# Attention steps of a head pair and one query tile, in a chain of two transformer blocks

## The chip, the core and the metric

The kernel runs on one core of a Trainium2 chip. Its engines are named as in the profile: PE (TensorE: matmuls and transposes; PEld is its loading of weights), DVE (VectorE), ACT (ScalarE), POOL (GpSimd) and SP (SyncE, which here only issues loads of weights). The metric is the time of one execution on the device in microseconds; less is better.

## The reference

Two blocks in a chain, all in fp32, D = 1024, batch 1. The first has 272 tokens (16 meta tokens and 256 of a 4 x 64 grid) and two layers, each a feed-forward part, a mixer, and another feed-forward part:

```
h = concat([meta, x])                                   # 16 + 256 tokens
for i in range(2):
    f1 = swiglu(rmsnorm(h, g[0]), gate, up, down);      h = h + 0.5 * rmsnorm(f1, g[1])
    hn = rmsnorm(h, g[2])
    m  = neighborhood_attention(hn) if i == 0 else diff_attention(hn)
    h  = h + rmsnorm(m, g[3])
    f2 = swiglu(rmsnorm(h, g[4]), ...);                 h = h + 0.5 * rmsnorm(f2, g[5])

def neighborhood_attention(h):                          # 16 heads of 64
    q, k, v = h @ w_qkv + b_qkv;  q = q * 64 ** -0.5
    # meta queries see the meta keys only
    om = softmax(qm @ km.T + meta_bias) @ vm
    # a grid query sees a window of 4 rows x 16 columns, and the meta keys
    og = softmax([q @ k_window.T + rpb, q @ km.T + meta_bias]) @ [v_window, vm]
    return concat([om, og]) @ w_o + b_o
```

The differential attention has 8 heads with two softmaxes each over all 272 keys; the values meet the difference of the two. The second block sees the 256 grid tokens. Its mixer computes, from one projection, attention with 8 heads of 64 in blocks of 256 keys, which for 256 tokens is plain causal attention, and beside it an mLSTM with 4 heads; an MLP with a squared ReLU follows.

## The kernel before

**Projections.** Activations lie transposed, features on the partitions and tokens in the columns. Each projection is made of products of 128 x 128 weights with 272 (or 256) columns, in three parts: high times high, low times high, high times low (`mm3`, L362 to L364). `Weights` brings the weights in: a raw load `wr` (SP), its high part `wh` (ACT, L122), and its low part `wl`, the difference of the two (L134), a *split* from here on, 128 x 1024 elements. The engine of the splits is `W.engine`. After each gemm, `W.pump()` issues up to two splits, and copies `wh` for later ones. `split` (L390) makes the high and low parts of an output in the same way, with the low part always on DVE.

**Mixers.** `mixer` runs the projections of q, k and v, two gemms per weight pair. The attention is a generator: it goes a piece further at k = 2 and k = 5 in each gemm and after each pump (`bg`). So the order of the code sets the order on every engine; the engines run it in order. A step u = (head pair, head) of `na_attention` does the following, for one head and both query tiles of 128:

- `scores(u)`: products of 64 partitions (the head's half) with 272 columns (L903), mask and row maximum on DVE (L856), exponentials on ACT;
- `weights(u)`: reciprocals of the sums and the scaling of the weights on DVE (L914, L915);
- `turn(u - 2)`: transposes on PE (L924) into PSUM, copied by ACT into `PT`, a ring of two buffers;
- `values(hp)`, every second step: the outputs of a head pair (L937), and before them those of its meta queries (L933), which wait for `ptm` (L981), the turned weights of the meta queries.

The meta queries of two head pairs are worked on together, one piece in each of three steps (`meta_scores`, `meta_weights` with L973, `meta_turn`). The window mask is added to the table of biases on POOL (`mask_bias`, 128 x 1536 elements a time). The products of projections, scores, values and half of the turns take turns in six PSUM buffers. `ready` tells `proj_out`, the output projection, which head pairs are complete.

The differential attention has its own steps (scores L1106, DVE L856, weights L1114 to L1118, values L1134, turned values `vs` L836). In the hybrid layer the order of gemms is written out as `plan`; `gates` (L1232, L1236) and the mLSTM run beside it, and `causal_attention` has the same steps as above: scores L1393, turns L1418, values L1426 to L1428; the query tile 0 sees 128 keys, the tile 1 sees 256. Rotary positions of q and k end in L1378 and L1379, the mLSTM's q in L1323.

**Engine of the splits.** It is POOL from the mixers' third gemm (`if 2 * n + q == 2`) and from the hybrid layer's `plan` on; `proj_out` sets it back to DVE (L652).

Of the kernel before, what the change touches and what calls it, by code (L numbers as in the profile page):

```python
# [13 lines left out]
AF = mybir.ActivationFunctionType  # L14
# [6 lines left out]
NM = 16  # L21
T = S + NM
# [153 lines left out]
def block_kernel(ctx: ExitStack, tc: tile.TileContext, a, out):  # L176
# [459 lines left out]
    def proj_out(post, x, order=range(8)):  # L636
# [15 lines left out]
        W.engine = dve  # L652
# [211 lines left out]
    ring = []  # L864
# [30 lines left out]
    def na_attention():  # L895
        vp, P, PT, em, ptm = {}, {}, {}, {}, {}
# [12 lines left out]

        def weights(u):  # L910
            for qt in range(2):
                e, sm = P[u, qt]
# [3 lines left out]
                P[u, qt] = e  # L916
# [467 lines left out]
    def causal_attention():  # L1384
        P, PT = {}, {}

        def scores(u):
            hp, b = divmod(u, 2)
            s = slice(64 * b, 64 * b + 64)
            for qt in range(2):  # L1390
# [4 lines left out]
                dve.tensor_tensor_reduce(out=lg[:, 0:n], in0=ps[:, 0:n], in1=causal[:, 256 - n:256], scale=1.0,  # L1395
# [5 lines left out]
                P[u, qt] = e, sm  # L1401

        def weights(u):
            for qt in range(2):
                n = 128 * (qt + 1)
                e, sm = P[u, qt]
# [3 lines left out]
                P[u, qt] = e  # L1410

        def turn(u):
            PT[u] = ring[0].tile()[:, 0:512].rearrange("p (k q) -> p k q", k=2)
            for qt in range(2):
                q = P.pop((u, qt))
                p = (ps_s if qt else ps_t)((128, 2, 128))
                for k in range(qt + 1):
                    pe.transpose(p[:, k, :], q[:, k * 128:k * 128 + 128], ident)  # L1418
                act.activation(PT[u][:, 0:qt + 1, qt * 128:qt * 128 + 128], p[:, 0:qt + 1, :], AF.Copy)
# [28 lines left out]
    W.engine = pool  # L1448
# [158 lines left out]
```

## Time and profile before

| | |
|---|---|
| median of 3 runs (lowest to highest) | 1474.24 us (1468.12 to 1475.06) |
| the profiled execution: own time, span | 1474.2 us, 1472.4 us |
| mean granted clock of PE | 0.991 |
| PE busy | 1438.7 us (98%), 10996 records |
| PEld busy | 1373.3 us (93%) |
| DVE busy | 907.2 us (62%), 1776 records |
| ACT busy | 752.8 us (51%) |
| POOL busy | 321.1 us (22%), 223 records |

The span runs from the first to the last instruction. Busy time is that in which an engine has a record running; a matmul of fp32 data leaves two records or more. The granted clock is a share of the full 2.4 GHz. 368 splits run on DVE (446.4 us) and 66 on POOL (159.9 us). The neighborhood mixer lies at about 243 to 352 us, the differential one at 815 to 927, the hybrid one at 1135 to 1265; nearly all the rest is feed-forward.

### The profile page before, as it was taken

What the parts mean: (1) busy time and instruction counts of PE and PEld (TensorE: products, weight loads), DVE (VectorE), ACT (ScalarE), POOL (GpSimd) and SP (SyncE); (2) the same over time, 40 slices, a digit from 0 to 9 for tenths busy, and PEclk for the clock granted to TensorE, in tenths of its full rate; (3) what the DMA queues carried; (4) which work ended last, traced back from release to release, by engine and by line L of the source; (5) the groups of instructions that cost most, each with busy time, mean ns of one, the idle gap of its engine ahead of it and who ended that gap; (6) DMA issues with size and microseconds to landing.
All of it is one profiled execution on the core that took longest, in us unless ns stands there. A gap on an engine that the chain in (4) does not pass through costs nothing.

```text
span 1472.4 us, 27036 instructions
## 1 busy us (share of the span) xinstructions
PE 1438.7 (98%) x10996; PEld 1373.3 (93%) x10996; DVE 907.2 (62%) x1776; ACT 752.8 (51%) x1327; POOL 321.1 (22%) x223
## 2 busy tenths in 40 slices
PE   9999999899999999999999899999999998999998
PEld 8999998788999999999999799999999887999886
DVE  6777448864775544765545755686645767596542
ACT  4554445555654444554444466564444555576541
POOL 3424002452021200121100455022200655000000
PEclk9999999999999999999999999999999899999999
DMA  7887554422385555265553433275554533265651
GB/s 235 253 250 202 171 183 129 116 86 87 93 269 177 171 175 193 90 226 172 166 179 115 146 113 115 87 230 188 178 186 137 173 115 112 90 193 183 213 188 40
DMA packets 231707, 236.42 MB, mean 161 GB/s; under 512 B 17825, under 2 KB 221798, under 8 KB 231390
## 3 DMA queue, kind: packets, MB, share of 16 engines
q1 hardware_dynamic: 230750, 229.63, 49.4%
q0 software_dynamic: 688, 4.99, 1.1%
q8 instruction: 87, 1.43, 0.4%
q14 instruction: 38, 0.31, 0.1%
q10 hardware_dynamic: 144, 0.07, 0.0%
HBM read 233.60 MB, written 5.13 MB: 162 GB/s over the span
## 4 chain that ended last, share of the span: by engine, by line
PE 74%; DVE 4%; ACT 1%; issue 0%; POOL 0%; DVEq 0%; POOLq 0%; ACTq 0%
PE pm L362 19%; PE pm L364 19%; PE pm L363 19%; PE ps L1531 2%; PE ps L1530 2%; PE ps L1532 2%; PE pm L475 2%; PE pm L471 1%; PE pm L472 1%; PE ps L1134 1%; PE pt L313 1%; PE ps L1106 1%; PE ps L937 0%; PE pm L445 0%; DVE hb L566 0%
## 5 line engine op out<-in xcount | busy, mean ns | idle before, releaser
L362 PE MATMUL pm<-xh,wh 128*128 128x272 f32 (+1 forms) x1992 | 584.2, 293 | 0.4 <-DVE s L856 0.4
L364 PE MATMUL pm<-xh,wl 128*128 128x272 f32 (+1 forms) x1992 | 572.1, 287 | 0.0
L363 PE MATMUL pm<-xl,wh 128*128 128x272 f32 (+1 forms) x1992 | 570.8, 287 | 0.0
L122 ACT ACTIVATE wh<-wr 128x1024 fp32r<-128x1024 f32 (+2 forms) x433 | 443.6, 1033 | 201.9 <-PE pm L363 121.8
L134 DVE TENSOR_TENSOR wl<-wr,wh 128x1024 fp32r<-128x1024 f32 (+2 forms) x368 | 446.4, 1221 | 123.9 <-ACT wh L122 123.0
L362 PEld LDWEIGHTS pm<-xh,wh 128*128 128x128 f32 x1992 | 378.3, 190 | 14.1 <-issue 10.9
L364 PEld LDWEIGHTS pm<-xh,wl 128*128 128x128 f32 x1992 | 378.0, 190 | 0.0
L363 PEld LDWEIGHTS pm<-xl,wh 128*128 128x128 f32 x1992 | 377.9, 190 | 0.1
L364 PE MATMUL pm<-mh,wl 128*128 128x272 f32 (+1 forms) x704 | 202.2, 287 | 0.0
L362 PE MATMUL pm<-mh,wh 128*128 128x272 f32 (+1 forms) x704 | 202.1, 287 | 0.0
L363 PE MATMUL pm<-ml,wh 128*128 128x272 f32 (+1 forms) x704 | 201.5, 286 | 0.0
L134 POOL TENSOR_TENSOR wl<-wr,wh 128x1024 fp32r<-128x1024 f32 x66 | 159.9, 2430 | 91.7 <-ACT wh L122 79.8
L599 POOL TENSOR_TENSOR sr<-sl,rb 128x272 f32<-128x272 f32 (+1 forms) x88 | 106.3, 1212 | 320.3 <-ACT sl L597 320.3
L364 PEld LDWEIGHTS pm<-mh,wl 128*128 128x128 f32 x704 | 132.6, 188 | 0.0
L363 PEld LDWEIGHTS pm<-ml,wh 128*128 128x128 f32 x704 | 132.6, 188 | 0.0
L362 PEld LDWEIGHTS pm<-mh,wh 128*128 128x128 f32 x704 | 132.5, 188 | 0.0
L318 POOL TENSOR_TENSOR s<-s,mhalf 128x3 f32<-128x3 f32 (+1 forms) x15 | 11.9, 796 | 504.8 <-DVE s L331 372.8
L389 ACT ACTIVATE mh<-m 128x272 fp32r<-128x272 f32 (+1 forms) x88 | 37.7, 428 | 120.5 <-DVE m L604 120.3
L604 DVE TENSOR_TENSOR m<-pm,sr 128x272 f32<-128x272 f32 (+1 forms) x88 | 38.2, 434 | 77.7 <-PE pm L364 72.0
L597 ACT ACTIVATE sl<-gq 128x272 f32<-128x272 f32 (+1 forms) x88 | 37.0, 428 | 89.3 <-DVE gq L595 88.7
L595 DVE TENSOR_TENSOR gq<-pm,rb 128x272 f32<-128x272 f32 (+1 forms) x88 | 37.5, 434 | 71.4 <-PE pm L364 63.6
L357 DVE TENSOR_TENSOR accf<-accf,sq 128x272 f32<-128x272 f32 (+1 forms) x42 | 18.3, 435 | 83.0 <-ACT sq L356 82.8
(343 smaller groups left out, 1912.0 us busy)
## 6 DMA issues: line engine op xcount, KB each, us to landing
wr<-in_ffn_w_gate_dram SPq DMA_DIRECT2D x43, 1024.0 KB
wr<-in_ffn_w_up_dram SPq DMA_DIRECT2D x43, 1024.0 KB
wr<-in_ffn_w_down_dram SPq DMA_DIRECT2D x32, 1024.0 KB
wr<-in_w_up_dram SPq DMA_DIRECT2D x16, 1024.0 KB
wr<-in_w_down_dram SPq DMA_DIRECT2D x16, 1024.0 KB
wr<-in_ffn_w_down_dram SPq DMA_DIRECT2D x16, 768.0 KB
wr<-in_na_w_qkv_dram SPq DMA_DIRECT2D x12, 1024.0 KB
wr<-in_da_w_qkv_dram SPq DMA_DIRECT2D x12, 1024.0 KB
```

The source lines that it names most:

```text
L122: self.nc.scalar.activation(hi, w, AF.Copy)
L134: engine.tensor_tensor(lo, w, hi.bitcast(F32), op=OP.subtract)
L362: pe.matmul(ps, wh[:, k, :], xh[:, j, cols], start=start, stop=False)
L363: pe.matmul(ps, wh[:, k, :], xl[:, j, cols], start=False, stop=False)
L364: pe.matmul(ps, wl[:, k, :], xh[:, j, cols], start=False, stop=stop)
L389: act.activation(hi, src, AF.Copy)
L475: pe.matmul(ps[q][:, c], w[q][0][:, k, :], norm.xl[:, k, c], start=False, stop=k == 7)
L595: dve.tensor_tensor(t[:, c], ps[:, c], norm.rb[:, c], op=OP.mult)
L597: act.activation(s[:, c], t[:, c], AF.Silu)
L599: pool.tensor_tensor(s2[:, c], s[:, c], norm.rb[:, c], op=OP.mult)
L604: dve.tensor_tensor(t[:, c], ps[:, c], gated.pop(f)[:, c], op=OP.mult)
L1530: pe.matmul(ps, xh, wh, start=start and k == 0, stop=False)
```

## The change

It does four things. (1) A step of `na_attention` and `causal_attention` is now u = (head pair, query tile): the products of the pair's two heads, which lie on partitions 0 to 63 and 64 to 127, stand next to each other, and `PT` holds one tile of both heads. (2) The values go tile by tile, the heads in turn: in the neighborhood layer twelve products of 128 columns where there were six of 256. (3) The outputs of the meta queries leave `values` and get a step of their own, `meta_values(g)`, with a split of their own; `part_done` marks a head pair ready after both. Their other pieces come one step later. (4) The three lines that set `W.engine` are gone, so that it stays DVE; of POOL's 66 splits 64 move there, and two in the first feed-forward stage, which name POOL themselves, stay.

```diff
-        W.engine = dve
...
+        def part_done(hp):
+            parts[hp] = parts.get(hp, 0) + 1
+            if parts[hp] == 2:
+                ready.add(hp)
 
         def scores(u):
-            hp, b = divmod(u, 2)
-            g = u // 4
-            for qt in range(2):
-                ps = ps_s()
-                pe.matmul(ps, kq[64 * b:64 * b + 64, hp % 4, QT[qt]], kq[64 * b:64 * b + 64, 4 + hp % 4, :],
-                          start=True, stop=True)
-                s0 = 2 - 2 * qt
-                e, r = softmax(ps, [(slice(0, NM), mb[:, u * NM:u * NM + NM]),
-                                    (GRID, bt[g][:, u % 4, s0:s0 + 4, :].rearrange("p s k -> p (s k)"))], T)
-                P[u, qt] = e, r
+            hp, qt = divmod(u, 2)
+            ps = [ps_s() for _ in range(2)]
+            for b in range(2):
+                s = slice(64 * b, 64 * b + 64)
+                pe.matmul(ps[b], kq[s, hp % 4, QT[qt]], kq[s, 4 + hp % 4, :], start=True, stop=True)
+            s0 = 2 - 2 * qt
+            for b in range(2):
+                hd = 2 * hp + b
+                bias = bt[hp // 2][:, hd % 4, s0:s0 + 4, :].rearrange("p s k -> p (s k)")
+                P[u, b] = softmax(ps[b], [(slice(0, NM), mb[:, hd * NM:hd * NM + NM]), (GRID, bias)], T)
...
         def turn(u):
-            PT[u] = ring[0].tile().rearrange("p (k q) -> p k q", k=3)
-            for qt in range(2):
-                q = P.pop((u, qt))
-                p = (ps_s if qt else ps_t)((128, 3, 128))
+            PT[u] = ring[0].tile().rearrange("p (b k q) -> p b k q", b=2, k=3)
+            for b in range(2):
+                q = P.pop((u, b))
+                p = (ps_s if b else ps_t)((128, 3, 128))
                 for i, x in enumerate((0, 128, 144)):
                     pe.transpose(p[:, i, :], q[:, x:x + 128], ident)
-                act.activation(PT[u][:, :, qt * 128:qt * 128 + 128], p, AF.Copy)
+                act.activation(PT[u][:, b], p, AF.Copy)
 
         def values(hp):
             o = ps_s()
-            v = vp.pop(hp)
-            for b in range(2):
-                s = slice(64 * b, 64 * b + 64)
-                i = 2 * (hp % 2) + b
-                pe.matmul(o[s, 0:NM], v[0:NM, 0, s], ptm[hp // 2][:, i * 16:i * 16 + 16], start=True, stop=True)
-            for k in range(3):
-                for b in range(2):
-                    s = slice(64 * b, 64 * b + 64)
-                    pe.matmul(o[s, NM:T], v[:, k, s], PT[2 * hp + b][:, k, :], start=k == 0, stop=k == 2)
-            split(Oh[:, hp, :], Ol[:, hp, :], o)
-            ready.add(hp)
+            for qt in range(2):
+                for k in range(3):
+                    for b in range(2):
+                        s = slice(64 * b, 64 * b + 64)
+                        pe.matmul(o[s, QT[qt]], vp[hp][:, k, s], PT[2 * hp + qt][:, b, k, :],
+                                  start=k == 0, stop=k == 2)
+            split(Oh[:, hp, GRID], Ol[:, hp, GRID], o[:, GRID])
+            part_done(hp)
...
+        def meta_values(g):
+            o = ps_s((128, 2, NM))
+            for n in range(2):
+                for b in range(2):
+                    s = slice(64 * b, 64 * b + 64)
+                    i = 2 * n + b
+                    pe.matmul(o[s, n, :], vp[2 * g + n][0:NM, 0, s], ptm[g][:, i * 16:i * 16 + 16],
+                              start=True, stop=True)
+            x = slice(2 * g, 2 * g + 2)
+            split(Oh[:, x, 0:NM], Ol[:, x, 0:NM], o)
+            for n in range(2):
+                part_done(2 * g + n)
+
         for u in range(16 + 3):
             if u % 2 == 0 and u >= 4:
                 values(u // 2 - 2)
@@ -989,13 +1004,15 @@
             if u < 16:
...
-                if u % 4 == 1:
+                if u % 4 == 2:
                     meta_scores(u // 4)
                 yield
-                if u % 4 > 1:
-                    (meta_weights, meta_turn)[u % 4 - 2](u // 4)
                 weights(u)
+                if u % 4 == 3:
+                    meta_weights(u // 4)
             yield from v_step(u)
+            if u >= 4 and u % 4 < 2:
+                (meta_turn, meta_values)[u % 4](u // 4 - 1)
...
-                if 2 * n + q == 2:
-                    W.engine = pool
...
         def scores(u):
-            hp, b = divmod(u, 2)
-            s = slice(64 * b, 64 * b + 64)
-            for qt in range(2):
-                n = 128 * (qt + 1)
-                ps = ps_s()
-                pe.matmul(ps[:, 0:n], qk[s, hp, QT[qt]], qk[s, 4 + hp, NM:NM + n], start=True, stop=True)
+            hp, qt = divmod(u, 2)
+            n = 128 * (qt + 1)
+            ps = [ps_s() for _ in range(2)]
+            for b in range(2):
+                s = slice(64 * b, 64 * b + 64)
+                pe.matmul(ps[b][:, 0:n], qk[s, hp, QT[qt]], qk[s, 4 + hp, NM:NM + n], start=True, stop=True)
+            for b in range(2):
...
         def values(hp):
             o = ps_s()
-            for b in range(2):
-                s = slice(64 * b, 64 * b + 64)
-                pt = PT[2 * hp + b]
-                pe.matmul(o[s, NM:NM + 128], vtok[:, hp, 0, s], pt[:, 0, 0:128], start=True, stop=True)
-                pe.matmul(o[s, NM + 128:T], vtok[:, hp, 0, s], pt[:, 0, 128:256], start=True, stop=False)
-                pe.matmul(o[s, NM + 128:T], vtok[:, hp, 1, s], pt[:, 1, 128:256], start=False, stop=True)
+            for qt in range(2):
+                for k in range(qt + 1):
+                    for b in range(2):
+                        s = slice(64 * b, 64 * b + 64)
+                        pe.matmul(o[s, QT[qt]], vtok[:, hp, k, s], PT[2 * hp + qt][:, b, k, :],
+                                  start=k == 0, stop=k == qt)
...
-    W.engine = pool
```

**DVE, neighborhood layer, between steps 0 and 1.** Before: the scaling of step 0's weights (L915), the evacuation of a projection (L879), then the masks and maxima of step 1 (L856).

```order
L914 RECIPROCAL s_2926<-s_2904 128x1
L915 TENSOR_SCALAR keep_2579<-keep_2579,s_2926 128x272
L914 RECIPROCAL s_2929<-s_2915 128x1
L915 TENSOR_SCALAR keep_2579<-keep_2579,s_2929 128x272
L879 TENSOR_TENSOR qkv_2938<-pm_2885,rb_2835 128x272
L856 ISA lg_2953,s_2954<-ps_2951,mb 128x16
L856 ISA s_2954 128x1
L856 ISA lg_2953,s_2956<-ps_2951,bt_1149,s_2954 128x256
```

After, in the same place (the lines are now L920, L878, L855):

```order
L919 RECIPROCAL s_2926<-s_2906 128x1
L920 TENSOR_SCALAR keep_2579<-keep_2579,s_2926 128x272
L919 RECIPROCAL s_2929<-s_2915 128x1
L920 TENSOR_SCALAR keep_2579<-keep_2579,s_2929 128x272
L878 TENSOR_TENSOR qkv_2938<-pm_2885,rb_2835 128x272
L134 TENSOR_TENSOR wl_2875<-wr_2768,wh_2874 128x1024
L134 TENSOR_TENSOR wl_2881<-wr_2768,wh_2880 128x1024
L855 ISA lg_2955,s_2956<-ps_2951,mb 128x16
L855 ISA s_2956 128x1
L855 ISA lg_2955,s_2958<-ps_2951,bt_1149,s_2956 128x256
```

Two splits now stand between step 0's weights and step 1's scores; each mixer step has one or two of them there.

**DVE, differential layer, between steps 0 and 1.** Before: weights (L1114 to L1118), evacuation (L1084), scores (L856).

```order
L1114 RECIPROCAL s_9623<-s_9603 128x1
L1115 RECIPROCAL s_9624<-s_9612 128x1
L1116 TENSOR_SCALAR keep_9298<-keep_9298,s_9623 128x272
L1117 TENSOR_TENSOR s_9624<-s_9624,nlam 128x1
L1118 SCALAR_TENSOR_TENSOR keep_9298<-keep_9298,s_9624 128x272
L1084 SCALAR_TENSOR_TENSOR kq_9295<-pm_9586,rb_9550 128x256
L856 ISA lg_9659,s_9660<-ps_9657,t_643_4874 128x272
L856 ISA s_9660 128x1
L859 TENSOR_SCALAR s_9662<-s_9660 128x1
```

After:

```order
L1129 RECIPROCAL s_9683<-s_9663 128x1
L1130 RECIPROCAL s_9684<-s_9672 128x1
L1131 TENSOR_SCALAR keep_9358<-keep_9358,s_9683 128x272
L1132 TENSOR_TENSOR s_9684<-s_9684,nlam 128x1
L1133 SCALAR_TENSOR_TENSOR keep_9358<-keep_9358,s_9684 128x272
L1099 SCALAR_TENSOR_TENSOR kq_9355<-pm_9646,rb_9610 128x256
L134 TENSOR_TENSOR wl_9638<-wr_9549,wh_9637 128x1024
L134 TENSOR_TENSOR wl_9644<-wr_9549,wh_9643 128x1024
L855 ISA lg_9719,s_9720<-ps_9717,t_647_4934 128x272
L855 ISA s_9720 128x1
L858 TENSOR_SCALAR s_9722<-s_9720 128x1
```

Only the two splits are added; the steps of this layer are as they were.

**PE, neighborhood layer, the first values.** Before: the end of a piece of a projection, the meta queries' outputs (L933), the values (L937), the turning of step 2 (L924).

```order
L362 MATMUL pm_3147<-xh_2573,wh_2858 128x272
L363 MATMUL pm_3147<-xl_2574,wh_2858 128x272
L364 MATMUL pm_3147<-xh_2573,wl_2859 128x272
L933 MATMUL ps_3179<-ptm_3162,bt_1149 64x16 x2
L937 MATMUL ps_3179<-ring_2778,bt_1149 64x256 x6
L924 MATMUL pt_3189<-ident,keep_2579 128x128 x3
L924 MATMUL ps_3194<-ident,keep_2579 128x128 x3
```

After (`...` leaves out projections; L981 turns the meta queries' weights, L834 the values of a head pair, L991 gives the meta queries' outputs):

```order
L362 MATMUL pm_3142<-xh_2573,wh_2858 128x272
L363 MATMUL pm_3142<-xl_2574,wh_2858 128x272
L364 MATMUL pm_3142<-xh_2573,wl_2859 128x272
L938 MATMUL ps_3172<-ring_2778,bt_1149 64x128 x12
L929 MATMUL pt_3186<-ident,keep_2579 128x128 x3
L929 MATMUL ps_3191<-ident,keep_2579 128x128 x3
...
L834 MATMUL pt_3252<-ident,bt_2779 128x128 x3
L981 MATMUL pt_3258<-ident,em_3060 16x16 x4
...
L991 MATMUL ps_3337<-ptm_3263,bt_1149 64x16 x2
L991 MATMUL ps_3337<-ptm_3263,bt_1298 64x16 x2
```

The values stand in the same place without the meta outputs ahead of them; the meta weights are turned later, and the outputs of two head pairs come another piece later.

## Rows read from the trace of the kernel before

**Rows 1.** Windows by stage: stretch, length, PE, PEld, DVE, ACT, POOL busy, clock, DMA, GB/s

```profile
243.00:352.00 109.00, 101.61 (x745) 85.32 (x744) 78.38 (x269) 66.09 (x158) 54.79 (x22) 0.98 0.44 125
390.00:590.00 200.00, 199.95 (x1587) 199.56 (x1586) 117.11 (x164) 96.22 (x140) 27.29 (x23) 1.00 0.56 182
815.00:927.00 112.00, 103.98 (x784) 94.58 (x784) 64.78 (x245) 59.99 (x159) 57.81 (x37) 0.97 0.38 123
1135.00:1200.00 65.00, 61.54 (x460) 58.45 (x460) 41.02 (x111) 36.58 (x64) 36.21 (x19) 0.92 0.44 135
1200.00:1265.00 65.00, 60.41 (x449) 53.14 (x449) 46.64 (x150) 32.59 (x95) 27.55 (x16) 0.97 0.29 94
245.00:270.00 25.00, 19.51 (x136) 15.86 (x136) 23.68 (x71) 16.14 (x38) 14.13 (x6) 0.99 0.75 202
```

**Rows 2.** Timeline of PE, score products: start, us, engine, line, operation

```profile
286.31 1.18 PE L903 MATMUL ps<-kq 64*128 64x272 f32 x4
848.45 0.73 PE L1106 MATMUL ps<-kq 64*128 64x272 f32 x4
1240.19 0.92 PE L1393 MATMUL ps<-qk 64*128 64x128 f32 x4
```

**Rows 3.** Timeline and source view (ns: least, median, most) of value products

```profile
283.30 1.52 PE L937 MATMUL ps<-ring,bt 128*64 128x256 f32 x12
1252.22 0.43 PE L1426 MATMUL ps<-ring,vtok 128*64 128x128 f32 x2
1252.98 0.38 PE L1428 MATMUL ps<-ring,vtok 128*64 128x128 f32 x2
L937 PEld LDWEIGHTS ps<-ring,bt x96: 132/137/226, 269.4 to 362.6; 128*64 128x64 f32 x96
```

**Rows 4.** Groups by line and form, 245 to 270 us: busy, mean ns, idle before

```profile
L915 DVE TENSOR_SCALAR keep<-keep,s 128x272 f32<-128x272 f32 x7 | 8.2, 1170 | 0.2
L134 DVE TENSOR_TENSOR wl<-wr,wh 128x1024 fp32r<-128x1024 f32 x3 | 3.6, 1217 | 0.0
L973 DVE TENSOR_TENSOR em<-em,rm 16x64 f32<-16x64 f32 x1 | 2.1, 2070 | 0.0
L134 POOL TENSOR_TENSOR wl<-wr,wh 128x1024 fp32r<-128x1024 f32 x6 | 14.5, 2437 | 13.8 <-ACT wh L122 13.8
```

**Rows 5.** Timeline of the neighborhood start; in brackets the wait before and its cause

```profile
268.07 2.35 POOL L134 TENSOR_TENSOR wl<-wr,wh 128x1024 fp32r<-128x1024 f32 x1 [2.94 <-ACT wh L122]
268.73 1.85 DVE L915 TENSOR_SCALAR keep<-keep,s 128x272 f32<-128x272 f32 x1
269.16 0.29 PE L933 MATMUL ps<-ptm,bt 16*64 16x16 f32 x4 [2.24 <-ACT ptm L981]
270.68 0.36 DVE L915 TENSOR_SCALAR keep<-keep,s 128x272 f32<-128x272 f32 x1
277.81 0.49 PE L924 MATMUL pt<-ident,keep 128*128 128x128 f32 x3
```

**Rows 6.** Timeline of the differential start

```profile
821.35 5.75 DVE L134 TENSOR_TENSOR wl<-wr,wh 128x1024 fp32r<-128x1024 f32 x2
827.01 0.43 DVE L856 CUSTOM_DVE_ANT_0 lg<-ps,t 128x272 f32<-128x272 f32 x1
837.54 0.42 DVE L856 CUSTOM_DVE_ANT_0 lg<-ps,t 128x272 f32<-128x272 f32 x1
839.26 0.36 ACT L836 ACTIVATE vs<-pt 128x256 f32<-128x256 f32 x1
839.68 1.65 PE L1134 MATMUL ps<-vs,ring 128*128 128x128 f32 x6 [3.65 <-ACT vs L836]
```

**Rows 7.** Waits of PE in the hybrid layer

```profile
1161.68 0.40 PE L1236 MATMUL pt<-ident,vtok 36*128 36x36 f32 x2 [3.32 <-DVE vtok L1232]
1232.72 0.47 PE L1418 MATMUL pt<-ident,mq 128*128 128x128 f32 x1 [2.50 <-DVE ry L1378]
```

**Rows 8.** Groups by line on DVE, 1200 to 1233 us

```profile
L390 DVE TENSOR_TENSOR Ol<-hy,Oh 128x256 fp32r<-128x256 f32 x4 | 6.9, 1720 | 0.0
```

More of the change, by code (lines that the diff above doesn't have):

```diff
@@ L895, in na_attention @@
     def na_attention():
-        vp, P, PT, em, ptm = {}, {}, {}, {}, {}
-        def scores(u):
-            hp, b = divmod(u, 2)
-            g = u // 4
-            for qt in range(2):
-                ps = ps_s()
-                pe.matmul(ps, kq[64 * b:64 * b + 64, hp % 4, QT[qt]], kq[64 * b:64 * b + 64, 4 + hp % 4, :],
-                          start=True, stop=True)
-                s0 = 2 - 2 * qt
-                e, r = softmax(ps, [(slice(0, NM), mb[:, u * NM:u * NM + NM]),
-                                    (GRID, bt[g][:, u % 4, s0:s0 + 4, :].rearrange("p s k -> p (s k)"))], T)
-                P[u, qt] = e, r
+        vp, P, PT, em, ptm, parts = {}, {}, {}, {}, {}, {}
+        def part_done(hp):
+            parts[hp] = parts.get(hp, 0) + 1
+            if parts[hp] == 2:
+                ready.add(hp)
+        def scores(u):
+            hp, qt = divmod(u, 2)
[8 more added lines that the diff above has]
+                P[u, b] = softmax(ps[b], [(slice(0, NM), mb[:, hd * NM:hd * NM + NM]), (GRID, bias)], T)
         def weights(u):
-            for qt in range(2):
-                e, sm = P[u, qt]
+            for b in range(2):
+                e, sm = P[u, b]
                 r = small([128, 1])
@@ L915, in weights @@
                 dve.tensor_scalar(e, e, r, None, op0=OP.mult)
[L916 removed]
+                P[u, b] = e
         def turn(u):
[L919 to L922 removed]
+            PT[u] = ring[0].tile().rearrange("p (b k q) -> p b k q", b=2, k=3)
+            for b in range(2):
+                q = P.pop((u, b))
+                p = (ps_s if b else ps_t)((128, 3, 128))
                 for i, x in enumerate((0, 128, 144)):
                     pe.transpose(p[:, i, :], q[:, x:x + 128], ident)
[L925 removed]
+                act.activation(PT[u][:, b], p, AF.Copy)
         def values(hp):
             o = ps_s()
[L929 to L939 removed]
+            for qt in range(2):
[6 more added lines that the diff above has]
+            part_done(hp)
         def turn_v(hp):
@@ L1387, in scores @@
         def scores(u):
-            hp, b = divmod(u, 2)
-            s = slice(64 * b, 64 * b + 64)
-            for qt in range(2):
-                n = 128 * (qt + 1)
-                ps = ps_s()
-                pe.matmul(ps[:, 0:n], qk[s, hp, QT[qt]], qk[s, 4 + hp, NM:NM + n], start=True, stop=True)
+            hp, qt = divmod(u, 2)
[5 more added lines that the diff above has]
+            for b in range(2):
                 lg, mx = tmp("lg"), small([128, 1])
-                dve.tensor_tensor_reduce(out=lg[:, 0:n], in0=ps[:, 0:n], in1=causal[:, 256 - n:256], scale=1.0,
+                dve.tensor_tensor_reduce(out=lg[:, 0:n], in0=ps[b][:, 0:n], in1=causal[:, 256 - n:256], scale=1.0,
                                          scalar=-3.0e38, op0=OP.add, op1=OP.max, accum_out=mx)
@@ L1400, in scores @@
                 act.activation(e[:, 0:n], lg[:, 0:n], AF.Exp, bias=nmx, scale=0.125, accum_out=sm)
-                P[u, qt] = e, sm
+                P[u, b] = e, sm
         def weights(u):
-            for qt in range(2):
-                n = 128 * (qt + 1)
-                e, sm = P[u, qt]
+            n = 128 * (u % 2 + 1)
+            for b in range(2):
+                e, sm = P[u, b]
                 r = small([128, 1])
@@ L1409, in weights @@
                 dve.tensor_scalar(e[:, 0:n], e[:, 0:n], r, None, op0=OP.mult)
-                P[u, qt] = e
+                P[u, b] = e
         def turn(u):
[L1413 to L1417, printed above, removed]
+            n = u % 2 + 1
+            PT[u] = ring[0].tile()[:, 0:512].rearrange("p (b k q) -> p b k q", b=2, k=2)
+            for b in range(2):
+                q = P.pop((u, b))
+                p = (ps_s if b else ps_t)((128, 2, 128))
+                for k in range(n):
                     pe.transpose(p[:, k, :], q[:, k * 128:k * 128 + 128], ident)
-                act.activation(PT[u][:, 0:qt + 1, qt * 128:qt * 128 + 128], p[:, 0:qt + 1, :], AF.Copy)
+                act.activation(PT[u][:, b, 0:n, :], p[:, 0:n, :], AF.Copy)
         def values(hp):
             o = ps_s()
-            for b in range(2):
-                s = slice(64 * b, 64 * b + 64)
-                pt = PT[2 * hp + b]
-                pe.matmul(o[s, NM:NM + 128], vtok[:, hp, 0, s], pt[:, 0, 0:128], start=True, stop=True)
-                pe.matmul(o[s, NM + 128:T], vtok[:, hp, 0, s], pt[:, 0, 128:256], start=True, stop=False)
-                pe.matmul(o[s, NM + 128:T], vtok[:, hp, 1, s], pt[:, 1, 128:256], start=False, stop=True)
+            for qt in range(2):
+                for k in range(qt + 1):
+                    for b in range(2):
+                        s = slice(64 * b, 64 * b + 64)
+                        pe.matmul(o[s, QT[qt]], vtok[:, hp, k, s], PT[2 * hp + qt][:, b, k, :],
+                                  start=k == 0, stop=k == qt)
             split(Oh[:, hp, c], Ol[:, hp, c], o[:, c])
```

## The prediction

> **What bounds the kernel now.** I read the busy shares first, then the windows by stage, then who waited for whom on TensorE (PE), then the timelines around the longest of those waits. In a feed-forward stage PE has no gap at all: 1587 records in 199.95 of 200 us, 0.126 us each [rows 1]. All of PE's idle time that this change can reach lies in the three mixers: 7.4 of 109 us in the neighborhood stage, 8.0 of 112 in the differential one, 3.5 + 4.6 of 130 in the hybrid one, 23.5 us together [rows 1]. The mean granted clock of those stretches is below 1 (0.98, 0.97, 0.92, 0.97), which is 2.2 + 3.4 + 5.2 + 2.0 = 12.8 us more, spent at the lower level of 1.2 GHz behind the longest waits [rows 1]. So the time is PE's own work plus, in the mixers, what VectorE (DVE) makes PE wait. From 245 to 270 us DVE is busy 23.7 of 25 us and PE 19.5: there DVE sets the pace [rows 1]. Much of DVE's busy time there is no work: a scaling of weights (L915) takes 0.36 us alone, 1.85 us when GpSimd (POOL) runs a split; it started at 268.73 and ended at 270.58, and the split ended at 270.42 [rows 5]. Its mean in the stretch is 1.17 [rows 4].
>
> **Score pairs.** The change puts the two heads of a pair, which lie on different halves of the partitions, next to each other. The differential stage already does that with the same shape, and its two products take 0.73 us against 1.18 us for two products on one half [rows 2]. The difference, 0.45 us, is one product's 272 columns, so 256 columns are 0.42 and 128 are 0.21, and the fixed part is 0.28: two products one after the other give 2 x 0.45 + 0.28 = 1.18, as measured, and the causal pair of 128 and 256 columns 0.21 + 0.42 + 0.28 = 0.91 against 0.92 [rows 2]. Neighborhood: 16 pairs x 0.45 = **7.2 us**. Causal: a head pair now costs 2 x 0.91; after it, (0.21 + 0.28) + (0.42 + 0.28) = 1.19; 0.63 less, times 4 = **2.5 us**.
>
> **Value products.** Neighborhood: six products of 256 columns become twelve of 128, two column halves in turn. Before, a head pair takes 1.52 us [rows 3], which is 3 x 0.42 + 0.26: two halves at once, bound by columns. Twelve of 128 columns are 6 x 0.21 + 0.26, the same. No row shows twelve short ones in strict turn. Bound below: no change; a gain is excluded, since the columns are the same. Bound above: the weight loads, 24 records of 137 ns one after the other [rows 3], 3.3 us, 1.8 us more for each of 8 head pairs, 14.4 us. I take no change, by the nearest row: the causal values are short products too, of which the two halves overlap only where one follows the other; their 12 records need 1252.22 to 1253.36, 1.14 us [rows 3], where 12 loads one behind the other would need 1.64, so loads do overlap. These causal products come into strict turn themselves: 3 x 0.21 + 0.26 = 0.89 against 1.14, times 4 = **1.0 us**. The Trainium skill speaks against the shorter products: TensorEngine Tiling, section Performance Considerations, gives each matmul an overhead of some 60 cycles and advises against cutting a dimension that is already small. By that page's figure the 48 added products, two records each, would cost an estimated 96 x 25 ns = 2.4 us; no run here shows it.
>
> **Splits on DVE.** 64 splits leave POOL (2.4 us each) for DVE (1.22 us each) [rows 4]. A split that DVE gains costs it 1.2 us; a split that POOL loses gives DVE back what it stood still for. In the first stretch: six splits [rows 4], 7.3 us, against 7 x (1.17 - 0.36) = 5.7 us on L915 alone [rows 4, 5] and some 3.7 us on two meta operations of about 2 us (L973 is one [rows 4]) that work 0.2 us each by their size. DVE's load there gets some 2 us lighter. In the new order a split stands one step behind the copy by ScalarE (wh) that it reads, so I count no wait for that. What is queued behind a split on DVE is the step's scores, and behind those PE's turning of the weights two steps later, so a delay of 1.2 us is covered in steady running: from the unstalled durations of the same stretch DVE needs about 0.4 (evacuation) + 1.2 + 1.6 (scores) + 0.95 (weights) + 0.5 (meta, low parts) = 4.7 us for a step, and PE 24 x 0.126 + 0.73 (scores) + 0.7 (turning) + 0.76 (half of a pair's values) = 5.2 us. It isn't covered where the mixer starts, so those places I follow by hand.
>
> Neighborhood start. DVE ends the weights of step 0 at 251.2 (it stood still to 253.5), of step 1 at 256.7, step 2 at 262.6, step 3 at 266.9 (before: 271.0, the end of the row at 270.68 [rows 5]). PE no longer waits for ptm ahead of the values (2.24 us [rows 5]), since the meta outputs have gone to their own step; it now waits some 2.9 us at the scores of step 3, whose PSUM buffers are those of step 2 that DVE reads until 261. It starts to turn step 3 at 270.3 instead of 277.81 [rows 5]: 7.5 us earlier, the first five score pairs among it. I write 7.3. The other 11 pairs give 11 x 0.45 = 4.9. Two later waits on the meta chain and on the mask (1.9 us of the 7.4) go in part, 1.2. Neighborhood: **13.4 us**. The mask additions stay on POOL and still stall DVE, 3.5 us each.
>
> Differential start. Only the splits change. Two splits on DVE took 5.75 us beside two on POOL [rows 6]; alone 2.35. Step 0's scores start at 823.7 instead of 827.01 [rows 6]; the weights end 2.8 us later; then an evacuation 0.33 and two splits 2.35, which POOL did before; so step 1 starts at 829.2 and step 2 at 834.7 instead of 837.54 [rows 6]. ScalarE's copy of the turned values (L836) stands behind step 2's exponentials, 1.72 us after their scores began; so PE's values start at 836.9 instead of 839.68 [rows 6]: **2.8 us**. The wait of 3.65 us there becomes longer, the one ahead of it goes, and the stretch at the low clock stays.
>
> Hybrid start. The gates: from 1154.6 DVE needs 3.2 us without POOL's stalls, two splits 2.35, then L1232 0.42: done at 1160.5, and PE, which waits for it, goes on at 1160.6 instead of 1161.68 [rows 7]: **1.1 us**. Before the first causal turn (wait 2.50 at 1232.72 [rows 7]) DVE loses, from 1200 on, 4 x 1.3 us of stalls on the low parts of the outputs [rows 8] and as much again on L1323 and L1379, 10.7 us in all, and gains seven splits, 8.5; half of that 2.2 reaches PE: **1.1 us**.
>
> Meta outputs: four more low-part subtractions and copies of 0.2 us, beside other work; their 16 products are the same number.
>
> **Sum.** 13.4 + 2.8 + (2.5 + 1.0 + 1.1 + 1.1) = 21.9. The profiled execution took 1474.2 us (span 1472.4 and 1.8 around it), the median of the runs is 1474.24, so they are one: 1474.2 - 21.9 = **1452 us**. I count no clock back: each start keeps a wait of over 2 us.
>
> **Rivals.**
> - All waits go, and the low clock with them: 7.2 + 2.5 + 1.0 of work, 23.5 of waits, 12.8 of clock: 1427. For it: every long wait is behind a DVE operation that POOL held up. Against it: DVE's load stays nearly the same, and the starts are bound by it. Partly so: 1427 to 1442.
> - The values are dearer, loads instead of columns: up to 14.4 us, 1456 to 1466. For it: no row shows strict turns at 128 columns; against it, the overlapping loads above. The page's overhead named above would end at the near end of this case.
> - DVE becomes the bound of the steps: its margin is 0.5 us of 5.2. If it needs 5.7 us a step over the 32 steps of the first two mixers, 16 us come back: 1463 to 1470, near no change. For it: its queue is in order and each wait for an exponential adds to the 4.7.
> - Slower: a split on DVE waits for ScalarE's wh and holds the scores behind it. POOL waited 2.3 us for it at each split (13.8 us for six [rows 4]). If DVE waited as long, a step would take 7.0 us against 5.2: 32 x 1.8 = 58 us, 1510. It decides from 1.4 us a split on (22 + 7.4 us over 32 steps, behind the margin of 0.5). Against it: POOL has nothing else to do and stands at the next split early; DVE comes there a step later. Half as long in one mixer would be no change.
> - The change doesn't do what it says: the pairs don't overlap in these stages. 7.2 + 2.5 come back: 1462. The differential pairs speak against it.
>
> **How the numbers follow.** About 0.5%, 7.4 us, is what this kernel's runs can tell from no change. Forecast, 1443 to 1461: 0.62. All waits go, or most: 0.12. Values dearer: 0.09. DVE the bound: 0.10. No overlap: 0.02. Slower: 0.05. Within 0.5% (1467 to 1482) lie the upper end of the dearer values where they meet a busier DVE (0.02), half of the DVE case (0.05) and the half-long waits (0.01): same 0.08. The rest of the last case is slower, 0.04, and all else faster, 0.88. The range, 1438 to 1466, leaves out two thirds of the second case (0.08), half of the DVE case (0.05) and the last (0.05), 0.18.
>
> **What would show it.** Neighborhood score pairs of 0.73 us and causal ones of 0.49 and 0.70; values at 1.5 us a head pair and 24 records; splits on DVE at 1.2 us and L915's line at 0.36 but beside the two mask additions; no PE wait for ptm, one for DVE at step 3; the differential values' wait longer than 3.65 us yet over by 837; mixers of about 96, 109 and 124 us. Wrong is the prediction if DVE's splits show waits for wh, if DVE is busy over 95% beyond the first 30 us of a mixer, or if the value records are 137 ns apart.

## The result, and the profile after

The changed kernel takes 1455.91 us in the median of 4 runs (1455.85 to 1458.19), against 1474.19 before: a ratio of 0.9887, with a 95% interval of 0.9871 to 0.9903. The profiled execution took 1455.85 us, span 1454.1. The page's busy times:

```profile
PE 1425.7 (98%) x11092; PEld 1366.7 (94%) x11092; DVE 931.7 (64%) x1844; ACT 754.0 (52%) x1331; POOL 167.2 (12%) x159
```

POOL has lost 154 us and DVE gained only 24.5, though its splits (L134) grew by 73.9, from 446.4 to 520.3 us: most of the other 49 is DVE's standing still beside POOL's splits, which went. To see where the 18.35 us between the two profiled executions lie, I cut both traces at the same instruction of each stage, the turn of the sums of squares (L313). Windows of the three mixer layers so cut (neighborhood, differential, hybrid), of before:

```profile
240.24:383.66 143.42, 136.03 (x1018) 117.05 (x1017) 92.39 (x300) 84.81 (x195) 55.64 (x23) 0.99 0.41 119
815.21:941.54 126.33, 118.31 (x906) 108.79 (x904) 74.02 (x256) 70.37 (x179) 57.81 (x37) 0.97 0.39 124
1152.18:1279.57 127.39, 119.48 (x889) 109.30 (x888) 81.93 (x243) 69.13 (x162) 63.06 (x33) 0.95 0.40 123
```

and of after:

```profile
238.58:376.63 138.05, 130.84 (x1113) 116.80 (x1112) 97.10 (x324) 86.23 (x199) 7.80 (x3) 0.98 0.43 124
808.17:931.90 123.73, 117.37 (x905) 108.09 (x904) 88.01 (x276) 70.35 (x179) 9.54 (x17) 0.97 0.39 126
1142.68:1261.19 118.51, 114.08 (x890) 104.54 (x888) 87.58 (x267) 68.48 (x162) 5.10 (x9) 0.97 0.43 132
```

In each line the second number is the length and the third PE's busy time. The layers gave 5.4, 2.6 and 8.9 us, 16.9 together. The feed-forward stages are the same within 0.1 us. The remaining 1.6 lie ahead of the first mark and are not the change's: the first transposes of the input, the same in both, took 0.69 us a pair in the execution before, and the first four pairs took 0.44 in the one after. That first stage takes 30.8 to 32.7 us in the profiles of all kernels below, and says nothing of them.

Products answer to [rows 2, 3]. Timeline of PE, a neighborhood score pair, its values, and in the hybrid layer the scores of both query tiles and the values:

```profile
275.20 0.73 PE L908 MATMUL ps<-kq 64*128 64x272 f32 x4
265.35 1.53 PE L938 MATMUL ps<-ring,bt 128*64 128x128 f32 x24
1219.71 0.49 PE L1409 MATMUL ps<-qk 64*128 64x128 f32 x4
1214.86 0.70 PE L1409 MATMUL ps<-qk 64*128 64x256 f32 x4
1235.29 0.88 PE L1445 MATMUL ps<-ring,vtok 128*64 128x128 f32 x12
```

Timelines of PE, then DVE, then POOL at the start of the neighborhood layer answer to [rows 5]:

```profile
253.34 0.25 PE L959 MATMUL ps<-kq 64*16 64x16 f32 x4 [1.30 <-DVE s L855]
254.15 0.27 PE L959 MATMUL ps<-kq 64*16 64x16 f32 x4 [0.56 <-DVE s L855]
255.65 0.59 PE L362 MATMUL pm<-xh,wh 128*128 128x272 f32 x1 [1.24 <-ACT ring L930]
273.65 0.55 PE L929 MATMUL pt<-ident,keep 128*128 128x128 f32 x3 [1.38 <-ACT bt L836]
250.23 2.35 DVE L134 TENSOR_TENSOR wl<-wr,wh 128x1024 fp32r<-128x1024 f32 x2
260.12 2.85 DVE L965 TENSOR_TENSOR lm<-lm,mx 16x64 f32<-16x64 f32 x1
278.60 3.33 DVE L920 TENSOR_SCALAR keep<-keep,s 128x272 f32<-128x272 f32 x1
259.43 3.47 POOL L721 TENSOR_TENSOR bt<-bt,misc 128x1536 f32<-128x1536 f32 x1 [19.00 <-DMA bt<-rpb_rows]
278.29 3.49 POOL L721 TENSOR_TENSOR bt<-bt,misc 128x1536 f32<-128x1536 f32 x1 [15.39 <-DMA bt<-rpb_rows]
```

PE's wait for `ptm` is gone, as forecast, but four others stand there. POOL's mask additions hold DVE (L965, a subtraction of 16 x 64, takes 2.85 us and 0.21 elsewhere), and they come earlier than before, at 259.4 and 278.3 us instead of 283.8 and 307.0: nothing stands ahead of them on POOL any more, and they wait only for the table's rows, which SP loads beside the weights. A window of those 10 us shows what goes with PE's waits from 252 to 256 us, a mean clock of 0.66:

```profile
252.00:262.00 10.00, 6.90 (x42) 6.71 (x41) 9.36 (x32) 5.45 (x13) 2.57 (x1) 0.66 0.80 224
```

Split by single microseconds it is 0.50, the level of 1.2 GHz, from 255 to 260, while PE, from 255.65 on, has products to run without a gap.

In the other two layers PE's waits answer to [rows 6, 7]:

```profile
829.54 0.80 PE L1149 MATMUL ps<-vs,ring 128*128 128x128 f32 x2 [5.15 <-ACT vs L835]
1151.08 0.28 PE L1251 MATMUL pt<-ident,vtok 36*128 36x36 f32 x2 [2.22 <-DVE vtok L1247]
1210.74 0.33 PE L1335 MATMUL pt<-ident,mq 128*128 128x128 f32 x1 [1.79 <-DVE mq L1329]
```

The wait of 2.50 us for `ry` ahead of the first causal turn is gone; the one for `mq`, 1.54 us before, stayed.

### The profile page after: what moved, and what is told of

It is laid out like the page before. It is cut to its first block, busy times and chain, and to the rows that moved or that the text cites. A ratio compares the mean times of both kernels' runs of the same rounds, so it can differ in the third digit from the quotient of the medians.

```text
span 1454.1 us, 27157 instructions
## 1 busy us (share of the span) xinstructions
PE 1425.7 (98%) x11092; PEld 1366.7 (94%) x11092; DVE 931.7 (64%) x1844; ACT 754.0 (52%) x1331; POOL 167.2 (12%) x159
## 4 chain that ended last, share of the span: by engine, by line
PE 71%; DVE 4%; ACT 1%; issue 0%; POOL 0%; DVEq 0%; POOLq 0%; ACTq 0%
PE pm L362 19%; PE pm L364 18%; PE pm L363 18%; PE ps L1548 2%; PE ps L1547 2%; PE ps L1549 2%; PE pm L475 2%; PE pm L471 1%; PE pm L472 1%; DVE wl L134 1%; PE ps L1149 1%; PE pt L313 1%; PE ps L1121 1%; DVE hb L566 0%; DVE xh L455 0%
## 5 line engine op out<-in xcount | busy, mean ns | idle before, releaser
L134 DVE TENSOR_TENSOR wl<-wr,wh 128x1024 fp32r<-128x1024 f32 (+1 forms) x432 | 520.3, 1212 | 123.5 <-ACT wh L122 122.5
L363 PEld LDWEIGHTS pm<-ml,wh 128*128 128x128 f32 x704 | 132.6, 188 | 0.0
L362 PEld LDWEIGHTS pm<-mh,wh 128*128 128x128 f32 x704 | 132.6, 188 | 0.0
L357 DVE TENSOR_TENSOR accf<-accf,sq 128x272 f32<-128x272 f32 (+1 forms) x42 | 18.3, 435 | 82.8 <-ACT sq L356 82.8
L860 ACT ACTIVATE keep<-lg,s 128x272 f32<-128x272 f32 x64 | 33.5, 524 | 47.4 <-DVE s L858 46.9
```

The lines of the kernel that those rows point to most:

```text
L134: engine.tensor_tensor(lo, w, hi.bitcast(F32), op=OP.subtract)
L362: pe.matmul(ps, wh[:, k, :], xh[:, j, cols], start=start, stop=False)
L363: pe.matmul(ps, wh[:, k, :], xl[:, j, cols], start=False, stop=False)
L860: act.activation(e[:, 0:n], lg[:, 0:n], AF.Exp, bias=nmx, accum_out=sm)
```

## The experiments

Eleven kernels were run. The table gives the median of each and, from its profiled execution, the lengths of the three layers, cut as above (us).

| kernel | median | neighborhood | differential | hybrid |
|---|---|---|---|---|
| before | 1474.2 | 143.4 | 126.3 | 127.4 |
| after | 1455.9 | 138.1 | 123.7 | 118.5 |
| e1 splits only | 1462.7 | 142.6 | 123.6 | 120.2 |
| e2 steps only | 1466.1 | 138.9 | 126.1 | 122.8 |
| e3 masks on DVE | 1455.2 | 136.3 | 124.3 | 118.5 |
| e4 values of 256 columns | 1456.6 | 139.1 | 124.2 | 118.6 |
| e5 e3, one split at first | 1446.8 | 134.0 | 119.0 | 116.8 |
| e6 e3, one split all along | 1458.5 | 134.5 | 120.7 | 118.6 |
| e7 e3, first value turns early | 1449.2 | 135.7 | 120.0 | 117.1 |
| e8 e5 and e7 together | 1443.4 | 132.6 | 117.6 | 116.5 |
| e9 e8, one split in hybrid too | 1440.5 | 132.6 | 117.5 | 114.2 |
| e10 e5, masks on POOL | 1449.3 | 137.4 | 119.1 | 116.7 |
| e11 e5, steps of before | 1455.2 | 137.3 | 119.3 | 119.8 |

The hybrid layer is the same program in after, e3 to e8 and e10, and differs there by 2.1 us; the low clock behind the gates goes with it (0.69 from 1152.5 to 1162.5 us in after, 118.5 us; 1.00 all through the layer in e5, 116.8). So a difference of 2 us in one layer of one execution can be clock alone.

### The change taken apart: e1 and e2

e1 is the kernel before without the lines that name POOL; e2 is the changed kernel with them.

```diff
-                if 2 * n + q == 2:
-                    W.engine = pool
...
-        W.engine = dve
...
-    W.engine = pool
```

> The kernel before with the three lines on the engine of the splits taken out, nothing else. If the prediction's sum holds part by part, this gives 5.0 + 1.2 us in the neighborhood layer (its start without the five score pairs), 2.8 in the differential one and 2.2 in the hybrid one: about 1463 us. If the two traces are read instead (neighborhood layer 5.4 us shorter although its score pairs alone give 7.2; hybrid layer 8.9 shorter, of which pairs and values 3.5), the splits lose some 2 us in the neighborhood layer and give 2.6 and 5.4 in the others: about 1468 us.

> The changed kernel with the splits on POOL again, so the new steps alone. By the prediction's sum 7.2 us (neighborhood pairs) and 3.5 (causal pairs and values): 1463.5 us. If the start of the neighborhood layer is set by DVE and not by PE's work, only the 11 pairs behind it count, 4.9 us, and the total is 8.4: about 1466 us. In neither case does the differential layer change.

Measured: 10.9 us for the splits and 7.4 for the steps, each against 1473.5 us of the kernel before on the same chip; together the 18.3 of the change. e1's total is the one that the prediction's sum gave, but not its parts: 0.9, 2.7 and 7.2 us by layer, for 6.2, 2.8 and 2.2. The errors cancel. e2 came out as expected of a start that DVE sets: 4.5, 0.2 and 4.6 us by layer. Windows of e1's neighborhood and hybrid layers:

```profile
238.35:380.92 142.57, 135.81 (x1017) 116.84 (x1016) 96.49 (x320) 86.05 (x195) 7.76 (x3) 0.98 0.42 120
1146.70:1266.94 120.24, 115.77 (x890) 105.80 (x888) 87.92 (x267) 68.98 (x162) 5.08 (x9) 0.99 0.42 130
```

In the hybrid layer PE's idle time fell from 7.9 to 4.5 us, as in after: the wait for `ry` is gone and that for the gates is 2.2, where e2 still has 3.0 and 3.3. The other 3.7 of e1's 7.2 us are PE's busy time at the same work, with a mean clock of 0.99 for 0.95; by layer, therefore, e1 and e2 do not add up there (7.2 and 4.6, for 8.9). In the neighborhood layer PE's idle time only fell from 7.4 to 6.8. Its largest part, the waits for `ptm`, was 2.8 in all before, and is now (PE's waits by cause: total, times, longest):

```profile
PE ps L932 <- ACT ptm L980: 4.0, 2, 3.3
```

With POOL free, its mask addition starts at 259.1 us and holds the meta queries' scaling (L972) for 2.48 us; `ptm` comes later, and the wait of 2.24 in [rows 5] is 3.28 here, with a mean clock of 0.98 for 0.99. How much of the missing 5.3 us each of these made up no run tells.

### The mask: e3 and e10

```diff
-    def mask_bias(g):
+    def mask_bias(g, engine=pool):
...
-        pool.tensor_tensor(t, t, window.unsqueeze(1).to_broadcast([128, 24, 64]), op=OP.add)
+        engine.tensor_tensor(t, t, window.unsqueeze(1).to_broadcast([128, 24, 64]), op=OP.add)
...
-            mask_bias(n // 4)
+            mask_bias(n // 4, dve)
```

> The changed kernel, with the two window-mask additions inside the neighborhood layer on DVE instead of POOL. Theory: POOL, which has no splits to do any more, adds the mask as soon as the data is there, at 259.4 us, and holds a DVE operation of the meta queries (L965) for 2.85 us where 0.21 would do, in the stretch that DVE paces; the second addition holds one for 3.3 us at 278.6. Without that the first turn behind the start (273.65) comes 2.6 us earlier and the wait of 0.97 us at 284 goes: 1452 to 1453.5 us, even with 2 x 1.8 us more work on DVE. Rival: the low clock of PE (254.5 to 260.9) is what the start lost, and that stays: no change, 1455 to 1457 us.

Measured: 1455.17 us (1454.64 to 1456.83), not to be told from the 1455.91 of after; the layer took 1.8 us less in the profile. The fourth turn of weights came 33.8 us behind the layer's mark instead of 35.1 (273.65 less 238.58), not 2.6 earlier, and the wait of 0.97 became 0.90. DVE no longer stands still (L965 takes 0.21 us), but it now waits for PE:

```profile
267.80 0.44 DVE L878 TENSOR_TENSOR qkv<-pm,rb 128x272 f32<-128x272 f32 x1 [0.97 <-PE pm L364]
```

And the low clock was shorter in this execution (0.69 from 255 to 260 us, for 0.50 in after), so e3 by itself doesn't tell what the stall cost from what the clock did. That left the waits at 253 to 256 us, and what sets them. e10 came later, with the splits of e5:

> The changed kernel with one split after each of the first eight gemms, and the masks on POOL as the change leaves them. Tells the mask from the splits: the mask's own share at the start was 1.8 us in the neighborhood layer with two splits a step; if it is the same here, 1448 to 1449 us; if the spare time of DVE hides the stall once it has fewer splits, as with the masks on DVE, 1446 to 1447 us.

Measured: 1449.30, and 3.4 us more in the layer than e5. PE's longest wait there is for the copy of values behind the held-up exponentials:

```profile
270.66 0.55 PE L929 MATMUL pt<-ident,keep 128*128 128x128 f32 x3 [2.94 <-ACT bt L836]
```

The turn comes 32.3 us behind the mark, for 30.0 in e5, both at the full clock up to there: 2.3 us for the stall, once the splits no longer hold the start. The rest of the 3.4 goes with the low clock behind this wait (0.82 from 270.66 to 280 us; e5 has 1.00 all through the layer).

### The values: e4

```diff
-            for qt in range(2):
-                for k in range(3):
...
+            both = ring[0].t[:, 0:1536].rearrange("p (t b k q) -> p t b k q", t=2, b=2, k=3)
+            for k in range(3):
...
+                    pe.matmul(o[s, GRID].rearrange("p (t q) -> p t q", t=2), vp[hp][:, k, s], both[:, :, b, k, :],
```

> The changed kernel, with the neighborhood values as six products of 256 columns again (the two query tiles read from the ring in one access). If columns set their time, as 1.53 us against 1.52 for a head pair says, no change: within 1 us of 1455.9. If each of the 48 added products had a cost of its own, as the Trainium skill has it (TensorEngine Tiling, Performance Considerations), an estimated 2.4 us less: 1453.5 us.

Measured: 1456.62 (1454.60 to 1458.90), no gain. Twelve products of 128 columns cost what six of 256 do: 24 records in 1.53 us, and their loads of 137 ns overlap. An overhead that each product adds, as the prediction read the Trainium skill (TensorEngine Tiling (Array Packing), Performance Considerations), doesn't show in this trace.

### The splits at the start, and the order of the copies: e5, e6, e7

e5 and e6, on top of e3 (e6 with 1 for every gemm of the two mixers), and e7, on top of e3 (in the differential layer for u == 2 alone; `v_step`, where these turns stood, leaves them out):

```diff
-                W.pump()
+                W.pump(1 if 2 * n + q < 8 else 2)
```

```diff
                 yield from available(u)
+                if u in (2, 4):
+                    turn_v(u // 2 - 1)
                 scores(u)
```

> The kernel with the masks on DVE, and in the first eight gemms of the neighborhood and differential mixers one split after each gemm instead of two; the splits left out follow later, two a step. Theory: at the start two splits in a row (2.35 us, three times) stand ahead of the scores on DVE, ACT's exponentials and copies wait behind those, and PE waits for PSUM buffers (1.30 + 0.56 + 1.25 us from 252 to 256) and then runs at the low clock until about 260. With one split a step PE's waits there shrink to under 1 us and the low clock goes: the neighborhood layer takes 132 to 134 us instead of 136.3, the total is 1451 to 1453. Rival: the load of DVE is the same and only its place changes; the waits come back where two splits a step follow: no change, 1454 to 1456.

> The same with one split after each gemm through the whole of both mixers. Theory: as before it, and no step later has two splits, so 1450 to 1453 us. Rival: the reserve of split weights stays short, and a gemm waits for its low part or for its raw load: 1456 us or more.

> The kernel with the masks on DVE, and the first turns of values (the step of index 2 in both mixers, and 4 in the neighborhood one) ahead of the step's scores in the order of the code, so that ACT's copies don't stand behind that step's exponentials. Theory: PE's wait of 5.15 us in the differential layer is for the place of the copy in ACT's queue, not for DVE: it falls below 2 us, that of 0.96 us at the fourth turn of the neighborhood layer goes, and the differential layer gets 2 to 5 us shorter: 1450 to 1453 us. Rival: DVE paces that stretch too, and PE waits as long at the next turn, for DVE's weights: no change, 1454 to 1456 us.

e5 measured 1446.77, better than its theory asked: besides 2.3 us in the neighborhood layer, the differential one gained 5.2 on e3 (2.9 of PE's idle time, and 2.3 of its busy time at the same work, with a mean clock of 1.00 for 0.97). Another 1.7 lie in the hybrid layer, which has the same program, and go with the clock (1.00 for 0.97 there too). PE of e5 at the start:

```profile
253.52 0.40 PE L362 MATMUL pm<-xh,wh 128*128 128x272 f32 x1 [1.25 <-ACT ring L930]
268.72 0.55 PE L929 MATMUL pt<-ident,keep 128*128 128x128 f32 x3 [0.95 <-ACT bt L836]
```

The meta queries' waits (1.30 and 0.56) are gone, and the fourth turn comes 30.0 us behind the mark. The clock of the same 10 us:

```profile
252.00:262.00 10.00, 8.75 (x85) 7.99 (x85) 8.89 (x40) 8.21 (x21) 0.00 (x0) 1.00 0.66 166
```

e6 met its rival: the low parts come too late, in the output projections (waits of 1.67 and 1.40 us) and in the feed-forward stages behind them, which are 1.5 and 1.7 us longer (PE's waits by cause):

```profile
PE pm L364 <- DVE wl L134: 5.2, 6, 1.7
```

e7 measured 1449.15: the wait of 5.15 us became

```profile
824.52 0.94 PE L1151 MATMUL ps<-vs,ring 128*128 128x128 f32 x6 [1.05 <-ACT vs L835]
```

so it was the copy's place in ACT's queue, behind exponentials that wait for DVE.

### Together, and the new steps without the splits' stalls: e8, e9, e11

e8 is e5 with e7's edit. e9 adds, in the loop over `plan`:

```diff
-        W.pump()
+        W.pump(1 if n < 6 else 2)
```

> Masks on DVE, one split after each of the first eight gemms, and the first turns of values ahead of the scores. Theory: the two waits are different (PSUM buffers at the scores, ACT's queue at the copy of the values), so most of both gains add: neighborhood layer 132.5 to 134, differential 117 to 119 us, total 1443 to 1446 us. Rival: both remove the same waits, so it is no better than one split alone, 1446 to 1448 us.

> The same, and in the hybrid layer one split instead of two after each of the gemms before the seventh. Theory: PE's wait of 2.2 us for the gates (L1247, two splits ahead of it on DVE) shrinks to 1 us and the low clock behind it with it: 2 to 4 us less than the run before. Rival: DVE has the splits to make up for later beside the causal steps and PE waits there: no change or 1 to 2 us more.

e8 measured 1443.44, as its theory had it: most of both gains add. e9 measured 1440.50 (1440.22 to 1440.69), a ratio to before of 0.9791 with 0.9776 to 0.9806: the fastest version here. Windows of the hybrid layer, e8 and e9:

```profile
1132.35:1248.87 116.52, 110.97 (x889) 101.51 (x888) 87.50 (x267) 68.29 (x162) 5.09 (x9) 1.00 0.43 134
1131.40:1245.63 114.23, 111.07 (x890) 101.71 (x888) 87.40 (x267) 67.83 (x162) 5.08 (x9) 1.00 0.44 137
```

e9's gain there is all waits, 2.4 us of PE's idle time; the low clock that its theory counted on had already gone in e8. Two waits behind the gates, 1.0 and 0.3 us, went, and the gates' own fell from 2.2 to

```profile
PE pt L1255 <- DVE vtok L1251: 1.0, 1, 1.0
```

e11 is the kernel before with e1's, e3's and e5's edits.

> The steps of the kernel before (head pair and head, meta outputs inside the values), with all splits on DVE, one split after each of the first eight gemms, and the masks on DVE: the run with one split, without the change's new steps. Their worth had been 4.5 us in the neighborhood layer beside splits that hold DVE, where the score pairs alone are 7.2. Theory: the rest was hidden by the start that DVE paced; with that start mended the new steps are worth 7 us or more there (141 us or more, against 134.0) and 3.5 in the hybrid layer: 1456 to 1459 us. Rival: part of the pairs' gain is lost all along the layer: 138 to 139.5 us, total 1453 to 1455.

Measured: 1455.21 (1451.59 to 1457.44), and 137.3 us in the neighborhood layer: the new steps are worth 3.3 us there, less than the rival had, and 3.0 in the hybrid layer. The layers are those of e11's fastest execution, 3.6 us below its median; where the other three lost more isn't known, but the total too lies next to the rival's 1453 to 1455. So the theory fell for the execution that was profiled. PE's waits of its layer are those for `ptm` alone; those of e5 are more and shorter:

```profile
PE ps L932 <- ACT ptm L980: 3.5, 2, 2.7
```

```profile
PE pt L929 <- ACT bt L836: 2.7, 4, 1.0
PE pm L362 <- DVE Ol L390: 1.4, 2, 0.9
PE pm L362 <- ACT ring L930: 1.3, 1, 1.3
```

Windows of the layer, e11 and e5:

```profile
238.28:375.60 137.32, 133.80 (x1017) 115.96 (x1015) 94.36 (x322) 86.13 (x195) 0.84 (x1) 1.00 0.43 124
```

```profile
238.73:372.75 134.02, 127.84 (x1113) 114.25 (x1112) 94.72 (x326) 86.17 (x199) 0.84 (x1) 1.00 0.44 127
```

PE's work is 6.0 us less, its idle time 2.7 more (6.2 against 3.5), at the full clock in both.

## Why the prediction was right, and where its parts were not

The time lay in the likeliest case's own range, 4 us above its middle. Point by point:

- **Score pairs, values.** 0.73, 0.49 and 0.70 us, and 1.53 and 0.88 for the values of a head pair, against 0.73, 0.49, 0.70, 1.5 and 0.89: right. The first refutes the rival "no overlap", the values and e4 refute "values dearer".
- **Splits on DVE.** 1.2 us each and no wait for `wh`, which refutes the slower rival. The group by line of after's neighborhood layer (29 splits in the differential and 31 in the hybrid layer stand the same, 0.0 us of wait):

```profile
L134 DVE TENSOR_TENSOR wl<-wr,wh 128x1024 fp32r<-128x1024 f32 x29 | 34.8, 1215 | 0.0
```

  Behind the start DVE is not the bound either: it is busy 15.1 of 20 us from 298 to 318.
- **Neighborhood start, 7.3 us: it gave 2.5** (the fourth turn 35.1 us behind the mark instead of 37.6). Two steps of the walk were wrong. "The mask additions stay on POOL and still stall DVE" took for granted that they stay in place; without splits ahead of them on POOL they moved into the stretch that DVE paces, 2.3 us at the fourth turn by e10 against e5 (1.3 by e3, where PE's clock differed too). And the wait at the start was put at the scores of step 3 with no price on the clock; it came at the meta queries' scores, because two splits in a row stand ahead of DVE's reading of the buffers, and PE then ran its next products at the lower level. With both mended the turn comes 30.0 us behind the mark (e5), where the prediction had it: 270.3 less 240.24 is 30.1.
- **Neighborhood, the rest, 4.9 + 1.2: it gave 2.9.** The score pairs did get 4.9 us shorter, but PE's busy time from the fourth turn on fell by 3.7, and its idle time rose from 1.9 to 2.7 instead of falling by 1.2. Windows of that part, before and after:

```profile
277.81:383.66 105.85, 103.95 (x801) 90.57 (x800) 62.28 (x211) 62.44 (x143) 38.58 (x16) 1.00 0.27 87
273.65:376.63 102.98, 100.25 (x886) 90.09 (x887) 67.01 (x227) 63.55 (x148) 3.49 (x1) 1.00 0.32 99
```

  The two waits of before (0.58 and 1.32) are gone, and PE now waits for DVE's low parts (0.97 and 0.52) and ACT's copies (0.55 the longest). That these had been in time for longer steps is argued from the waits; no run tests it by itself, and why PE's other records took 1.2 us more is open. e11 against e5 shows the same at the full clock, 6.0 us of work for 3.3.
- **Differential layer, 2.8: 2.6.** The wait ahead of the values became longer (5.15) and the one ahead of it went, as forecast; that wait ends at 829.54, which with the marks' shift of 7.04 is 836.6 in the time of before; 836.9 was forecast.
- **Hybrid layer, 5.7: 8.9.** Scores 2.5, values 1.0 (four times 1.14 less 0.88) and gates 1.1 (3.32 to 2.22) are right. "Half of that 2.2 reaches PE" was too little: the wait of 2.50 ahead of the causal turn went whole, and it went in e1 and not in e2, so the splits set it. PE's idle time fell by 3.5 us in all, from 7.9 to 4.4; what is left of 8.9 beyond that and the products is 1.9 us, which the clock can account for: behind `ry` (0.83 before from 1232 to 1242, 1.00 after from 1222.5 to 1232.5), and behind the gates.
- **"I count no clock back"** was wrong in both directions: it was lost at the neighborhood start (mean of the layer 0.99 before, 0.98 after) and won in the hybrid layer (0.95 and 0.97).

The sum came near partly by luck: the neighborhood layer fell short by 8 us, and the hybrid layer's 3.2 beyond the forecast and the 1.6 of the program's start, which is chance, made up for 4.8 of them.

Left open: which part of the low clock's stretches is chance. Their length differed between runs of the same instructions, so the layers of single executions above hold it as well.

## What to carry to other kernels

When work leaves an engine, whatever stays in its queue runs earlier; look up where, and whom it then holds. A wait that PE keeps costs more than its length if PE has work of its own right behind it and the clock has fallen; take the wait away at its root, which here was not how much DVE had to do but that two splits stood ahead of the scores. Shorter products on the bound engine are worth their time only as far as the copies behind them on the other engines can follow: at the full clock, about half of it in the two executions compared here.

## What the runs showed of the hardware

While POOL adds 128 x 1536 elements (3.47 us), a DVE operation of 16 x 64 elements, 0.21 us alone, takes 2.85 and ends with POOL's; one of 128 x 272, 0.36 alone, takes 3.33. By the Trainium skill (SBUF — State Buffer, Who interferes with whom) a DVE instruction with two inputs from SBUF and a GpSimd one that reads SBUF hold each other off for a whole instruction; the trace agrees, L965 ending at 262.97 us and POOL's addition at 262.90. Weight loads of products on different halves of the columns overlap: 24 records in 1.53 us whose loads of 137 ns would take 3.29 one after the other. The same transposes at the program's start ran at 0.69 or 0.44 us a pair from one execution to the next, and that stage's length differed by up to 1.9 us. In the execution after they went from 0.44 to 0.69 where the granted clock fell to 0.50 (8.3 to 15 us); in the one before the profile shows no low clock there, so whether it is the clock stays open. In the hybrid layer, the same instructions took 118.5 us with a mean clock of 0.97 and 116.8 with 1.00.
